# A two-layer hybrid trunk on one core: ten groups of output columns as seven products of quarters, the mixed rows kept as fp32 in DRAM, and weight scales on GpSimd

## The chip, the cores and the metric

The kernel runs on one core of a Trainium2 chip, as one launch. The metric is the device time of that launch in microseconds (us), lower is better. It is the median of 1742.44 us over three runs (1742.14 to 1742.74). The engines are named as the profile names them: PE (TensorE, matmul) with PEld for its weight loads, DVE (VectorE), ACT (ScalarE), POOL (GpSimd) and SP (SyncE, which issues most DMAs).

## The reference

512 tokens with 2048 features go through two layers. Each layer normalises the tokens, makes one combined input projection of 7696 columns, runs three branches on pieces of it, multiplies each branch by its own SiLU gate, joins the three (512 + 1024 + 512 = 2048 columns) and adds one output projection to the residual.

```python
def _layer(x, norm_g, w_in, conv_w, ..., w_out):
    h = _rmsnorm(x, norm_g)
    proj = h @ w_in                                   # 512 x 7696
    y_conv = _short_conv(...) * silu(cv_g)            # 512 columns
    q, k = _rmsnorm(sb_q), _rmsnorm(sb_k)             # 8 heads of 128
    y_sb = _stick_breaking(q, k, v) * silu(sb_g)      # 1024 columns
    g = log_sigmoid(gl_lr @ gla_w_up + gla_b_up) / 16
    y_gla = _rmsnorm(_gla(q, k, v, g)) * silu(gl_g)   # 512 columns
    mix = concatenate([y_conv, y_sb, y_gla])
    return x + mix @ w_out                            # w_out: 2048 x 2048

# stick breaking, per head and block of 128 queries
z = q @ k.T / sqrt(128)
log_keep = where(mask, log_sigmoid(-z), 0)
later = reverse_cumsum(log_keep) - log_keep
w = where(mask, exp(log_sigmoid(z) + later), 0)
out = w @ v
```

The result must be close to fp32. Every large product is therefore made of three fp16 products: with a = a_hi + a_lo and b = b_hi + b_lo, a·b is taken as a_hi·b_hi + a_hi·b_lo + a_lo·b_hi. The halves are fp16, and a power of two per tensor (or per block) brings them into range first.

## The kernel before

**Weight groups.** `specs` lists 76 groups of 256 weight columns in the order in which they are used: per layer 30 of the input projection (six for GLA, four for the first half of the convolution, four each for the four pairs of attention heads, four for the second half of the convolution) and 8 of the output projection. Everything is a pipeline over that list. `weights()` takes the group that PE will use now, lets SP fetch the group after next (`fetch`: two halves of 1 MB, fp32, into the `stage` pool) and prepares the next one (`load_`): ACT squares each half and sums it (`wmax`, L319), GpSimd adds the sums over the partitions (`wgm`, L329), DVE makes a power of two of that in four to six operations on one column (`wscale`, L330 to L350), ACT writes the high half `wh` in fp16 (L392), and DVE writes the rest `wl` (L399). Two 16-bit tiles per half, three halves in the pool.

**Matmuls of a group.** `project_toks` (L568 to L570 are its sister by columns, L576 to L578 the matmuls by tokens) keeps a block of 128 tokens x 128 features as the stationary operand and streams 256 weight columns: 4 token tiles x 16 feature blocks x 3 products = 192 matmuls of 256 columns in one group. `project_cols` gives 96 matmuls of 512 columns. Both use two PSUM banks of `psp`, which has three. The last group of each layer goes token tile by token tile (`project_by_token`, L601), as do the two GLA value groups.

**Branches.** While PE works on a group, ACT, DVE and GpSimd do the branch of earlier groups. GLA comes first and leaves most work to DVE. In attention, one iteration of the loop over j handles two heads and four groups (V, gate, Q, K). The scores and values of pair j are put into `later` and are called one by one between the groups of pair j+1 (`go()`). Per chunk of 128 x 896 or 128 x 384 scores, DVE runs L958, L959, the running sums L962, L965 and L970. `gate` (L609 to L620) copies a PSUM bank to SBUF on ACT first, and so frees the bank.

**Mix.** Each branch result is split into fp16 halves at once (`mixsplit`, L647 and L648) with a scale of its own branch, into two tiles `mh`, `ml`. The output weights then take eight ratios of scales (`wsr`, L347), so each half of a group's weights is made in four pieces of 128 x 512.

**Output groups.** Group `gi` takes the residual rows (`rt`), adds the scaled PSUM bank to them (L1078), writes the sum and, in layer 0, sums its squares on ACT (L1084) for the next layer's norm. The transposed fp16 tokens of the next layer come from `xprep`, as the last group's token tiles land.

**Order.** In the first 40 us the order on DVE and ACT is the program's own. After that a scheduler with a model of the times sets the order on each engine once, when the kernel is built; `high_priority` and `issue_after` are hints to it. On the chip, each engine runs its list in that order and waits for semaphores.

Of the kernel before, what the change touches and what calls it, by code (L numbers as in the profile page):

```python
# [17 lines left out]
P = 128  # L18
EPS = 1e-6
TAU = 16.0  # L20
XBITS = 8.0
RED = bass_isa.ReduceOp

# [7 lines left out]
CHUNKS = ((((3, 0), (2, 512)), (3, 2)), (((0, 0), (1, 128)), (0, 1)))  # L31


@with_exitstack
def hybrid_trunk(ctx, tc, x, norm_g, w_in, conv_w, conv_b, sb_qn_g, sb_kn_g,
# [10 lines left out]
    GX = GW + LR  # L46
    NG = D // GW
# [37 lines left out]
    xs = dram.tile([seq, D], F32, tag="xs", name="xs")  # L85
    xt = [newbig("x", [P, 2, D], F32) for _ in range(2)]
# [22 lines left out]
    parno = wk([P, 32], "raw", 1)  # L109
# [39 lines left out]
    r = 0  # L149
# [90 lines left out]

    V.tensor_scalar(xsc.bitcast(I32), xun.bitcast(I32), -1.0, float(254 << 23), ALU.mult, ALU.add)
# [30 lines left out]
    specs = []  # L272
    for l in range(depth):
        for cols in ([(GL_V, GW)], [(GL_V + GW, GW), (GL_LR, LR)], [(GL_Q, GW)], [(GL_K, GW)],
                     [(GL_G, GW)], [(GL_G + GW, GW)]):
            specs.append((l, w_in, cols))
        conv = [[(l, w_in, [(c0 + j * GW, GW)]) for c0 in (CV_H, CV_C, CV_G, CV_B)] for j in range(2)]
        specs += conv[0]
        for j in range(4):
            for c0 in (SB_V, SB_G, SB_Q, SB_K):  # L280
                specs.append((l, w_in, [(c0 + j * GW, GW)]))
        specs += conv[1]
        for gi in range(NG):
            specs.append((l, w_out, [(gi * GW, GW)]))
# [10 lines left out]
    def junk(n):  # L295

        return wk([P, HK * GX], "junk", 1, dt=U8)[:, :n]


    def fetch(i):  # L300

        l, src, cols = specs[i]
        staged[i] = st = []
        for h in range(2):
            s_ = stage.tile([P, HK, GX], F32, tag="st", name=nm("st"))
            o = 0
            for c0, w in cols:
                nc.sync.dma_start(
                    s_[:, :, o:o + w],
                    src[l, h * HK * P:(h + 1) * HK * P, c0:c0 + w].rearrange("(k p) n -> p k n", p=P))  # L310
                o += w
            st.append(s_)

    def wmax(i, h):

        n = sum(c[1] for c in specs[i][2])
        if h == 0:
            peak[i] = sm(2, "wm")
        S.activation(junk(HK * n).rearrange("p (k n) -> p k n", k=HK), staged[i][h][:, :, :n], AF.Square,  # L319
                     accum_out=peak[i][:, h:h + 1])  # L320

    def wscale(i):

        l, src, cols = specs[i]

        m = sm(1, "wq")
        if i:
            gm = sm(2, "wgm")
            G.partition_all_reduce(gm, peak.pop(i), P, RED.add)  # L329
            V.tensor_scalar(m, gm[:, 0:1], gm[:, 1:2], 2.0 ** -120, ALU.add, ALU.max)  # L330
        else:
# [5 lines left out]
            V.tensor_scalar(m, ps, 2.0 ** -120, None, ALU.max)  # L337
        V.tensor_scalar(m.bitcast(I32), m.bitcast(I32), 0x7F000000, None, ALU.bitwise_and)
        sc = sm(1, "ws")
        V.tensor_scalar(sc.bitcast(I32), m.bitcast(I32), -0.5, float(204 << 23), ALU.mult, ALU.add)  # L340
        p2 = sm(1, "wp")
        V.tensor_scalar(p2.bitcast(I32), m.bitcast(I32), 0.5, float(50 << 23), ALU.mult, ALU.add)
        u = sm(1, "wu", bufs=6)
        sw = None
        if src is w_out:
            sw = sm(8, "wsr")
            V.tensor_scalar(sw, ratio[l][0], sc, None, ALU.mult)  # L347
            V.tensor_tensor(u, p2, ratio[l][1], ALU.mult)
        else:
            V.tensor_tensor(u, p2, xun[:, l:l + 1], ALU.mult)  # L350
        loaded[i] = ([], u)
        scales[i] = (sc, sw)

    def wparts(i, h):
        sc, sw = scales[i]
        return [(slice(2 * j, 2 * j + 2), sw[:, h * 4 + j:h * 4 + j + 1]) for j in range(4)] \
            if sw is not None else [(slice(0, HK), sc)]
# [13 lines left out]

    def whi0(h, q, eng):

        if q == 0:
            wh = wpool.tile([P, HK, GX], F16, tag="wh", name=nm("wh"))
            wl = wpool.tile([P, HK, GX], F16, tag="wl", name=nm("wl"))
            loaded[0][0].append((wh, wl))
        wh = loaded[0][0][h][0]
        ks = slice(q * (HK // 2), (q + 1) * (HK // 2))
        if eng is S:  # L380
            S.activation(wh[:, ks, :GW], staged[0][h][:, ks, :GW], AF.Copy, scale=scales[0][0])
        else:
            V.tensor_scalar(wh[:, ks, :GW], staged[0][h][:, ks, :GW], scales[0][0], None, ALU.mult)

    lasthi = {}

    def whi(i, h):
        n = sum(c[1] for c in specs[i][2])
        wh = wpool.tile([P, HK, GX], F16, tag="wh", name=nm("wh"))
        wl = wpool.tile([P, HK, GX], F16, tag="wl", name=nm("wl"))  # L390
        for ks, s_ in wparts(i, h):
            lasthi[i] = S.activation(wh[:, ks, :n], staged[i][h][:, ks, :n], AF.Copy, scale=s_)  # L392
        loaded[i][0].append((wh, wl))
# [735 lines left out]
```

## Time and profile before

| | us |
|---|---|
| median of three runs (range) | 1742.44 (1742.14 to 1742.74) |
| span of the profiled execution, clock 1.00 throughout | 1740.9 |
| PE busy | 1726.8 (99%) |
| PEld busy | 1232.4 (71%) |
| ACT busy | 1090.0 (63%) |
| DVE busy | 1068.9 (61%) |
| POOL busy | 75.1 (4%) |
| DMA | 204.7 MB, 118 GB/s |

The span is cut by time into GLA (40 to 280 us), attention and second half of the convolution (280 to 735), output groups (735 to 880), the change of layers (880 to 900), and the same again to the end. The table of groups gives a line's busy time, its count and the mean time of one; matmuls are pipelined, so the mean of one (273 ns for 256 columns) is not the spacing of two. The spacing is read from a long stream in the chain of waits.

### The profile page before, as it was taken

To read this page: it belongs to the slowest core of one execution; us is meant where nothing else is said; L and a number is where in the kernel's file an instruction comes from. 1 tells how busy PE (TensorE), PEld (TensorE's weight loads), DVE (VectorE), ACT (ScalarE), POOL (GpSimd) and SP (SyncE) were. 2 spreads that over 40 slices of the span, in tenths; PEclk is the share of its full clock that TensorE was granted. 3 is DMA by queue.
4 is the path that set the end of the run, shared out by engine and by line. 5 is a ranking of instruction groups with operands and counts; after the bars stand their busy time and mean duration, and the time that the engine had idled before them with its cause. 6 is when DMAs were issued, how large, how long until landed. Compare 5 with 4: busy or idle time off the path is not lost.

```text
span 1740.9 us, 30651 instructions
## 1 busy us (share of the span) xinstructions
PE 1726.8 (99%) x12846; PEld 1232.4 (71%) x12846; DVE 1068.9 (61%) x2015; ACT 1090.0 (63%) x1460; POOL 75.1 (4%) x104
## 2 busy tenths in 40 slices
PE   8999999999999999999999999999999999999999
PEld 6744556868787754788885455668686868448888
DVE  7556788657665747433474576976575666673431
ACT  7558577667575867455555684766767667663540
POOL 1000000000000000000010000000000000000000
PEclk9999999999999999999999999999999999999999
DMA  6333313335353545444463333133454444453531
GB/s 222 121 97 97 98 58 113 103 104 131 108 140 110 128 121 128 134 158 146 138 148 105 97 97 97 50 121 110 125 124 109 117 124 126 112 132 113 177 124 40
DMA packets 266121, 204.69 MB, mean 118 GB/s; under 512 B 93106, under 2 KB 265212, under 8 KB 265472
## 3 DMA queue, kind: packets, MB, share of 16 engines
q1 hardware_dynamic: 256976, 193.29, 39.0%
q10 hardware_dynamic: 9008, 9.45, 1.6%
q8 instruction: 100, 1.64, 0.4%
q14 instruction: 37, 0.30, 0.1%
HBM read 173.36 MB, written 8.39 MB: 104 GB/s over the span
## 4 chain that ended last, share of the span: by engine, by line
PE 48%; issue 7%; DVE 1%; DMA 1%; SPq 0%; POOL 0%; ACT 0%; POOLq 0%; DVEq 0%
PE psp L576 8%; PE psp L578 8%; PE psp L577 8%; PE psp L570 6%; PE psp L568 6%; PE psp L569 6%; PE psp L601 3%; PE psz L749 1%; PE psm L988 1%; PE psz L944 1%; PE psz L840 0%; DMA m<-raw 0%; DVE wl L399 0%; SPq L487 0%; DMA xs<-x 0%
## 5 line engine op out<-in xcount | busy, mean ns | idle before, releaser
L577 PE MATMUL psp<-wl,m 128*128 128x256 f16 x1664 | 454.0, 273 | 0.0
L578 PE MATMUL psp<-wh,m 128*128 128x256 f16 x1664 | 453.9, 273 | 0.0
L576 PE MATMUL psp<-wh,m 128*128 128x256 f16 x1664 | 453.8, 273 | 0.0
L399 DVE SCALAR_TENSOR_TENSOR wl<-st,ws,wh 128x2048 f16<-128x2048 f32 (+1 forms) x120 | 282.3, 2353 | 193.1 <-ACT wh L392 179.7
L392 ACT ACTIVATE wh<-st,ws 128x2048 f16<-128x2048 f32 (+1 forms) x118 | 236.3, 2003 | 202.6 <-PE psp L569 100.9
L319 ACT ACTIVATE junk<-st 128x2048 uint8<-128x2048 f32 (+1 forms) x150 | 285.5, 1903 | 7.6 <-DMA st<-in_w_out_dram 4.5
L577 PE MATMUL psp<-wl,x 128*128 128x256 f16 x768 | 209.5, 273 | 0.0
L578 PE MATMUL psp<-wh,x 128*128 128x256 f16 x768 | 209.5, 273 | 0.0
L576 PE MATMUL psp<-wh,x 128*128 128x256 f16 x768 | 209.4, 273 | 0.0
L570 PE MATMUL psp<-m,wl 128*128 128x512 f16 x512 | 194.4, 380 | 0.0
L568 PE MATMUL psp<-x,wh 128*128 128x512 f16 x512 | 194.4, 380 | 0.0
L569 PE MATMUL psp<-x,wh 128*128 128x512 f16 x512 | 194.4, 380 | 0.0
L569 PE MATMUL psp<-m,wh 128*128 128x512 f16 x512 | 194.4, 380 | 0.0
L568 PE MATMUL psp<-m,wh 128*128 128x512 f16 x512 | 194.4, 380 | 0.0
L570 PE MATMUL psp<-x,wl 128*128 128x512 f16 x512 | 194.3, 380 | 0.0
L570 PEld LDWEIGHTS <-wl 128*128 128x128 f16 x1024 | 100.1, 98 | 122.8 <-issue 3.7
L569 PEld LDWEIGHTS <-wh 128*128 128x128 f16 x1024 | 100.1, 98 | 117.5 <-issue 1.1
L568 PEld LDWEIGHTS <-wh 128*128 128x128 f16 x1024 | 100.1, 98 | 115.3 <-issue 0.5
L576 PEld LDWEIGHTS <-m 128*128 128x128 f16 x1664 | 162.7, 98 | 19.9 <-issue 0.7
L578 PEld LDWEIGHTS <-m 128*128 128x128 f16 x1664 | 162.6, 98 | 19.4 <-issue 0.5
L577 PEld LDWEIGHTS <-m 128*128 128x128 f16 x1664 | 162.6, 98 | 18.8
L392 ACT ACTIVATE wh<-st,wsr 128x512 f16<-128x512 f32 x128 | 81.6, 710 | 100.5 <-PE psp L578 74.4
(285 smaller groups left out, 2260.4 us busy)
## 6 DMA issues: line engine op xcount, KB each, us to landing
st<-in_w_in_dram SPq DMA_DIRECT2D x120, 1024.0 KB, 5.3
st<-in_w_out_dram SPq DMA_DIRECT2D x32, 1024.0 KB, 5.5
x<-in_x_dram SPq DMA_DIRECT2D x4, 1024.0 KB
qT<-in_x_dram ACTq DMA_DIRECT2D x8, 512.0 KB, 5.3
qT<-xs ACTq DMA_DIRECT2D x8, 512.0 KB
xs<-x SPq DMA_DIRECT2D x14, 256.0 KB, 4.5
out_dram<-kT SPq DMA_DIRECT2D x14, 256.0 KB, 3.7
th<-za SPq DMA_TRANSPOSE x64, 3.6
```

What stands on the lines that cost most here:

```text
L319: S.activation(junk(HK * n).rearrange("p (k n) -> p k n", k=HK), staged[i][h][:, :, :n], AF.Square, accum_out=peak[i][:, h:h + 1])
L392: lasthi[i] = S.activation(wh[:, ks, :n], staged[i][h][:, ks, :n], AF.Copy, scale=s_)
L399: V.scalar_tensor_tensor(wl[:, ks, :n], staged[i][h][:, ks, :n], s_, wh[:, ks, :n], ALU.mult, ALU.subtract)
L568: T.matmul(o, wh[:, kk, cs], xh[:, :, k, :], start=st_, stop=False)
L569: T.matmul(o, wh[:, kk, cs], xl[:, :, k, :], start=False, stop=False)
L570: T.matmul(o, wl[:, kk, cs], xh[:, :, k, :], start=False, stop=en)
L576: T.matmul(o, ah[:, t, k, :], wh[:, kk, :n], start=st_, stop=False, skip_group_check=True)
L577: T.matmul(o, ah[:, t, k, :], wl[:, kk, :n], start=False, stop=False, skip_group_check=True)
L578: T.matmul(o, al[:, t, k, :], wh[:, kk, :n], start=False, stop=en, skip_group_check=True)
L601: T.matmul(o[:, :n], a_[:, t, k, :], w[k // HK][part][:, k % HK, :n], start=i == 0 and k == 0, stop=i == 2 and k == KT - 1)
L749: T.matmul(o, src16[sb][a][:, ss], tgt16[tb][b][:, g0:g1].rearrange("p g h c -> p (g h c)"), start=i == 0, stop=i == 2)
L944: T.matmul(z[:, o:o + (t + 1) * P], qT[:, a_, t, hh, :], kT[:, b_, :t + 1, hh, :], start=i == 0 and o % 512 == 0, stop=False, skip_group_c ...
```

## The change

**Seven products.** In both layers the output groups 2 to 6 are computed as 2 x 2 blocks: 256 tokens x 1024 features on the left, 1024 features x 128 columns on the right. With sums of the blocks on both sides, seven block products give what eight did. One product is 2 token tiles x 8 feature blocks x 3 fp16 products = 48 matmuls of 128 columns, a group is 336 of them.

- `right(i)` makes seven weight tiles from the staged fp32 quarters a, b, c, d: four sums or differences on DVE (128 x 1024 each, in place), and for each tile the high half on ACT and the rest on DVE.
- `mix_sums` makes, once per layer, four left-hand sums from the fp32 mix, and their halves.
- `seven` runs the products and combines them on the way out of PSUM, with two temporaries (`u2`, `vv`) and one copy (`s1`).

```diff
+SEVEN = {"gla": (), "conv0": (), "sb": (), "conv1": (), "out": (2, 3, 4, 5, 6)}
...
-    stage = ctx.enter_context(tc.tile_pool(name="stage", bufs=3))
-    wpool = ctx.enter_context(tc.tile_pool(name="wpool", bufs=3))
-    big = ctx.enter_context(tc.tile_pool(name="big", bufs=4))
+    stage = ctx.enter_context(tc.tile_pool(name="stage", bufs=4))
+    wpool = ctx.enter_context(tc.tile_pool(name="wpool", bufs=6))
+    big = ctx.enter_context(tc.tile_pool(name="big", bufs=2))
...
+    def right(i):
...
+        part(a)
+        V.tensor_tensor(b, b, d, ALU.add)
+        V.tensor_tensor(a, a, b, ALU.add)
+        part(a)
+        part(c)
+        V.tensor_tensor(c, c, a, ALU.add)
+        V.tensor_tensor(a, a, d, ALU.subtract)
+        part(a)
+        part(b)
+        part(d)
+        part(c)
...
+        product(o1, 0, True, False)
+            S.activation(s1, o1[:, :2 * P], AF.Copy, scale=ev.unit)
+        product(o2, 1, True, True)
+            ev.add(u2, o2[:, :2 * P], s1)
+        product(o1, 2, False, True)
+        ev.first(o1[:, :2 * P])
+        product(o3, 3, True, True)
+            ev.sub(vv, o3[:, :2 * P], u2)
+        product(o4, 4, True, False)
+        ev.last4(vv, o4[:, :2 * P])
+        product(o2, 5, True, True)
+        ev.plus(0, 1, o2[:, :2 * P], vv)
+        product(o4, 6, False, True)
+        ev.plus(1, 0, o4[:, :2 * P], u2)
```

On DVE, in layer 0, this is the work of about half an output group (group 4 before, group 4 after). First before: the lower halves of the weights, eight pieces, and the group's two evictions.

```order
L399 SCALAR_TENSOR_TENSOR wl_8339<-st_8066,wsr_8335,wh_8338 128x2x256 [waits DMAHW6_49,Activation_49]
L399 SCALAR_TENSOR_TENSOR wl_8339<-st_8066,wsr_8335,wh_8338 128x2x256 [waits Activation_49] x3
L399 SCALAR_TENSOR_TENSOR wl_8349<-st_8068,wsr_8335,wh_8348 128x2x256 [waits DMAHW7_49,Activation_49]
L399 SCALAR_TENSOR_TENSOR wl_8349<-st_8068,wsr_8335,wh_8348 128x2x256 [waits Activation_49] x3
L1078 SCALAR_TENSOR_TENSOR x_7557<-psp_8358,wu_8084,qT_8314 128x2x256 [waits DMAHW5_49,PE_49]
L1078 SCALAR_TENSOR_TENSOR x_7558<-psp_8359,wu_8084,qT_8314 128x2x256 [waits PE_49]
```

After, on DVE: `st` are the staged weights (L433 is the first sum b + d of the next group, L434 the second), `w` the lower halves, and L1340 to L1362 the combinations on the way out of PSUM.

```order
L433 TENSOR_TENSOR st_8495<-st_8495,st_8497 128x8x128 [waits DMAHW6_49,DMAHW5_49,Activation_49]
L1360 TENSOR_TENSOR qT_8903<-u_1003_9048,qT_8903 128x2x128 [waits DMAHW4_49,DVE_49]
L430 SCALAR_TENSOR_TENSOR w_8526<-st_8085,ws_8509,w_8526 128x1024 [waits Activation_49]
L430 SCALAR_TENSOR_TENSOR w_8529<-st_8085,ws_8509,w_8529 128x1024 [waits Activation_49]
L1348 SCALAR_TENSOR_TENSOR x_7581<-psp_8948,wu_8511,qT_8903 128x2x128 [waits PE_49]
L430 SCALAR_TENSOR_TENSOR w_8532<-st_8087,ws_8509,w_8532 128x1024 [waits Activation_49]
L430 SCALAR_TENSOR_TENSOR w_8535<-st_8087,ws_8509,w_8535 128x1024 [waits Activation_49]
L1343 SCALAR_TENSOR_TENSOR vv_9148<-psp_9099,wu_8511,u_1003_9048 128x256 [waits PE_49]
L1354 TENSOR_TENSOR qT_8903<-vv_9148,qT_8903 128x2x128 [waits DVE_49]
L1360 TENSOR_TENSOR qT_8903<-vv_9148,qT_8903 128x2x128
L1356 SCALAR_TENSOR_TENSOR x_7582<-psp_9150,nu_9199,qT_8903 128x2x128 [waits DVE_49,PE_49,Pool_49]
```

The first sum of the next group (L433) now stands ahead of the lower halves of the present one, and it waits for ACT, which squares the next group's weights; before, nothing on DVE stood between a group's lower halves and its evictions.

**Weight scales on GpSimd.** The five operations on one column move from DVE to GpSimd, with fp32 arithmetic in place of the bit mask. Before, on DVE, for one output group:

```order
L330 TENSOR_SCALAR wq_8325<-wgm_8326 128x1 [waits Pool_49]
L338 TENSOR_SCALAR wq_8325<-wq_8325 128x1 [waits DVE_49]
L340 TENSOR_SCALAR ws_8330<-wq_8325 128x1 [waits DVE_49]
L342 TENSOR_SCALAR wp_8332<-wq_8325 128x1
L347 TENSOR_SCALAR wsr_8335<-ratio_7385,ws_8330 128x8 [waits DVE_49]
L348 TENSOR_TENSOR wu_8334<-wp_8332,rgm_7380 128x1 [waits DVE_49]
```

After, on POOL, for one output group. [...]

```order
L348 ISA
L348 ISA wgm_9325<-wm_9319 128x2 [waits Activation_49]
L352 ISA
L352 TENSOR_SCALAR wq_9324<-wgm_9325 128x1 [waits Pool_49]
L361 TENSOR_SCALAR wq_9324<-wq_9324 128x1 [waits Pool_49]
L363 TENSOR_SCALAR ws_9329<-wq_9324 128x1 [waits DVE_49,Pool_49]
L365 TENSOR_SCALAR wu_9331<-wq_9324,rub_7378 128x1
L1352 TENSOR_SCALAR nu_10006<-wu_9331 128x1 [waits DVE_49,Pool_49]
```

POOL's list grows from 109 rows to 610, with one change of library before the change and 154 after it.

```diff
     def wscale(i):
...
-            V.tensor_scalar(m, gm[:, 0:1], gm[:, 1:2], 2.0 ** -120, ALU.add, ALU.max)
+            E = G
+            E.tensor_scalar(m, gm[:, 0:1], gm[:, 1:2], 2.0 ** -120, ALU.add, ALU.max)
...
-        V.tensor_scalar(m.bitcast(I32), m.bitcast(I32), 0x7F000000, None, ALU.bitwise_and)
+        E.tensor_scalar(m, m.bitcast(I32), 2.0 ** -24, MAGIC, ALU.mult, ALU.add)
...
+        E.tensor_scalar(sc.bitcast(I32), m, -(2.0 ** 23), (MAGIC + 204) * 2.0 ** 23, ALU.mult, ALU.add)
```

**Mix in DRAM.** `spill` writes each branch row block (128 x 512 fp32, 256 KB) to `mixd` in DRAM; `mix_load` brings twelve of the sixteen back before the last projection of the layer, and the last four stay in SBUF. `mix_unit` makes one scale for all, `mix_split` the fp16 halves, into the same two tiles that held the normalised tokens. With one scale, the ratios `wsr` and their eight pieces per group go.

```diff
-    def mixsplit(k, y, s_, t0=0):
...
+        def spill(k, y):
+            nc.sync.dma_start(mixd[k], y)
...
+        LATE = (10, 11, 2, 3)
+        for k in (0, 4, 6, 8, 12, 14, 10, 2):
+            mix_split(k, s_)
+        if any(modes[cursor[0]:cursor[0] + NG]):
+            sums = mix_sums(s_)
```

**Attention.** The running sum now takes both terms, so per chunk DVE runs one scan per query tile and two operations instead of four. The values of the second head of pair j move by one iteration (`held`).

```diff
-                    V.scalar_tensor_tensor(w, w, -1.0, a, ALU.mult, ALU.subtract)
-                    V.scalar_tensor_tensor(a, z[:, :zw], zs, w, ALU.mult, ALU.subtract)
-                    for t, o in qtiles:
-                        back = a[:, o:o + (t + 1) * P][:, ::-1]
-                        V.tensor_tensor_scan(back, ones.to_broadcast([P, (t + 1) * P]), back, 0.0,
-                                             ALU.mult, ALU.add)
-                    V.tensor_tensor(w[:, :zw - 1], w[:, :zw - 1], a[:, 1:], ALU.subtract)
+                    for t, o in qtiles:
+                        grow_, keep_ = (x[:, o:o + (t + 1) * P][:, ::-1] for x in (w, a))
+                        V.tensor_tensor_scan(keep_, grow_, keep_, 0.0, ALU.add, ALU.add)
+                    V.scalar_tensor_tensor(w, z[:, :zw], zs, a, ALU.mult, ALU.subtract)
...
+            prior = held.pop() if held else lambda: None
+            if j < 3:
+                held.append(lambda: values(1))
+                later.extend((lambda: scores(0), prior, lambda: scores(1), lambda: values(0)))
```

On ACT, at the start of the third pair of heads (j = 2), layer 0. Before, the two banks of V leave PSUM (L1011) ahead of the softmax of the pair before:

```order
L1011 ACTIVATE v_4965<-psp_4771 128x512 [waits PE_49]
L392 ACTIVATE wh_5045<-st_4743,ws_5039 128x8x256 [waits DVE_49,PE_49]
L1011 ACTIVATE v_4965<-psp_4772 128x512
L952 ACTIVATE za_4984<-psz_4975,zun 128x896 [waits DMAHW7_49,PE_49]
L956 ACTIVATE zw_4988<-psz_4975,nzun 128x896
```

After, they leave (L1233) behind the softmax (L1171 to L1183) and behind the first column block of the gate (L809):

```order
L1180 ACTIVATE zw_4974<-zw_4974 128x896 [waits DVE_49]
L809 ACTIVATE ga_5138<-psp_5038,nu_5136 128x512 [waits PE_49]
L1183 ACTIVATE za_4970<-zw_4974 128x896 [waits Activation_49]
L1233 ACTIVATE v_4953<-psp_4759 128x512 [waits PE_49]
L1233 ACTIVATE v_4953<-psp_4760 128x512
L811 ACTIVATE ga_5138<-ga_5138 128x512 [waits DVE_49]
```

L1233 waits for PE: the tile `v` has two buffers, and the held values of pair j-2 still read the older one.

**Gate.** `gate` takes exp, ln and exp from the PSUM bank (three ACT operations for five) and multiplies from the bank too (L813), so a bank is held until DVE's last operation on it.

More of the change, by code (lines that the diff above doesn't have):

```diff
@@ L519, in hybrid_trunk @@
     xlow(0, 1, mix, True)
-    wlo(0, 0)
-    wlo(0, 1)
+    for q in range(4):
+        wlo(0, q)
     xhigh(1, 0, mix)
@@ new lines, in project_toks @@
+    def project_toks(late=()):
+        w, u = weights()
+        ps = [bank(psp, "p") for _ in range(2)]
+        rounds = [[k for k in range(h * HK, (h + 1) * HK) if k not in late] for h in range(2)] + [list(late)]
+        lastk = [q for q in rounds if q][-1][-1]
+        for ks in rounds:
+            for t in range(NT):
+                o = ps[t // 2][:, (t % 2) * GW:(t % 2 + 1) * GW]
+                for k in ks:
+                    wh, wl = (wview(w, i, k, GW) for i in range(2))
+                    T.matmul(o, xh[:, k, t, :], wh, start=k == 0 and t % 2 == 0, stop=False, skip_group_check=True)
+                    T.matmul(o, xh[:, k, t, :], wl, start=False, stop=False, skip_group_check=True)
+                    T.matmul(o, xl[:, k, t, :], wh, start=False, stop=k == lastk, skip_group_check=True)
+        return ps, u
@@ new lines, in project_by_token, with quarters, own @@
+    def project_by_token(n):
+        w, u = weights()
+        for t in range(NT):
+            o = bank(psp, "p")
+            for i, (a_, part) in enumerate(((xh, 0), (xl, 0), (xh, 1))):
+                for k in range(KT):
+                    T.matmul(o[:, :n], a_[:, k, t, :], wview(w, part, k, n),
+                             start=i == 0 and k == 0, stop=i == 2 and k == KT - 1)
+            yield t, o, u
+    def quarters(sums):
+        def own(th, kh):
+            return [a[:, kh * HK:(kh + 1) * HK, 2 * th:2 * th + 2, :] for a in mix]
+        return own(0, 0), sums[1], own(0, 1), sums[0], sums[2], sums[3], own(1, 1)
```

597 lines of the change are left out of this document (384 added, 213 removed).

## The prediction

> **What bounds the kernel now.** I read the page's busy times first, then the windows by stage, then the chain of waits for the spacing of matmuls, and last the timeline of one output group.
>
> ```profile
> PE 1726.8 (99%) x12846; PEld 1232.4 (71%) x12846; DVE 1068.9 (61%) x2015; ACT 1090.0 (63%) x1460; POOL 75.1 (4%) x104
> PEclk9999999999999999999999999999999999999999
> ```
>
> ```profile
> 280.00:700.00 420.00, 420.00 (x3161) 303.39 (x3160) 275.15 (x468) 283.43 (x351) 19.51 (x26) 1.00 0.45 118
> 735.00:860.00 125.00, 125.00 (x1147) 111.92 (x1146) 48.45 (x99) 67.33 (x123) 2.39 (x6) 1.00 0.51 161
> 880.00:900.00 20.00, 17.22 (x156) 15.10 (x154) 17.54 (x29) 11.49 (x16) 3.91 (x2) 1.00 0.63 130
> 1720.00:1740.90 20.90, 17.29 (x159) 15.24 (x156) 1.94 (x4) 0.00 (x0) 0.00 (x0) 0.99 0.08 26
> ```
>
> PE is busy for 1726.8 of 1740.9 us, at full clock. In the windows (span, PE, PEld, DVE, ACT, POOL) it has no gap in attention (420 of 420 us) nor in the output groups (125 of 125); it stands still for 2.8 us at the change of layers and 3.6 us in the last window, the rest at the start. So time falls only where PE has less to do, and rises wherever another engine makes PE wait. Work taken from DVE or ACT is worth nothing by itself.
>
> ```profile
> 1015.49 1.34 PE psz L749 x24
> 1160.34 3.32 PE psz L840 x48
> 1228.90 0.65 PE psz L944 x3
> 1229.61 0.49 PE psz L944 x3
> 1274.29 1.65 PE psm L988 x18
> 1716.33 20.97 PE psp L601 x192
> 1737.33 0.48 DVE kT L1078
> ```
>
> The chain gives spacings: 192 matmuls of 256 columns take 20.97 us, 109.2 ns each. 24 matmuls of 128 columns take 1.34 us, 55.8 ns each. The 48 of L840 are 36 of 128 columns and 12 of 256, and 36 × 55.8 + 12 × 109.2 ns = 3.32 us agrees. Matmuls of 512 columns come every 0.216 us (thirteen steps between these two rows of the timeline), 48 of them take 10.4 us:
>
> ```profile
> 299.81 0.38 PE L569 MATMUL psp<-x,wh 128*128 128x512 f16 x1
> ...
> 302.62 0.38 PE L570 MATMUL psp<-x,wl 128*128 128x512 f16 x1
> ```
>
> **Seven products: the gain.** 336 × 55.8 ns = 18.75 us against 20.97 us, 2.22 us per group. Ten groups: **-22.2 us**. That the spacing holds over 336 matmuls rather than 24 is not in the trace; it is the first thing that can fail (rival A).
>
> **Seven products: what else must fit into 18.75 us.**
>
> ```profile
> L1054 DVE SCALAR_TENSOR_TENSOR qp<-raw,qp 128x1024 f16<-128x1024 f32 x16 | 19.6, 1226 | 18.0 <-ACT qp L1053 18.0
> L1053 ACT ACTIVATE qp<-raw 128x1024 f16<-128x1024 f32 x16 | 16.9, 1057 | 44.0 <-DVE raw L1049 25.8 <-DVE raw L1044 18.1
> L319 ACT ACTIVATE junk<-st 128x2048 uint8<-128x2048 f32 (+1 forms) x150 | 285.5, 1903 | 7.6 <-DMA st<-in_w_out_dram 4.5 <-DMA st<-in_w_in_dram 1.2
> L995 DVE SCALAR_TENSOR_TENSOR e<-psm,vu,g 128x256 f32<-128x256 f32 x32 | 13.9, 476 | 0.0
> L735 DVE TENSOR_TENSOR m<-e,m 128x256 f16<-128x256 f32 x32 | 13.4, 423 | 7.8 <-ACT m L734 7.3
> L1084 ACT ACTIVATE junk<-x 128x256 uint8<-128x256 f32 x32 | 13.3, 416 | 65.8 <-DVE x L1078 65.0 <-ACT junk L1084 0.3
> ```
>
> DVE: 11 operations of 128 x 1024 (seven lower halves, four sums) at 1.23 us, six evictions at 0.48 and three small sums at 0.42, together 17.6 us; neighbours in the timeline overlap by about 0.09 us, so about 15.8. ACT: seven high halves at 1.06, two squares of weights at 1.90 and their read-outs at 0.19, `s1` and, in layer 0, four squares of the result at some 0.6, together 12 to 14.4. Both fit, DVE with 1 to 3 us to spare. What counts is the order. From group 3 on, DVE's sum b + d of the next group stands ahead of the lower halves of tiles 4 to 7 of the present one, and it waits for ACT's square of the next weights. From the start of a group: product 1 ends at 48 × 55.8 ns = 2.68 us, `s1` 0.42, a square 0.5 (layer 0), the weights' square 2.1, the sum 1.22, a small sum 0.33, the lower half 1.14: 8.4 us, where product 4 wants that tile at 3 × 2.68 = 8.04. So PE waits about 0.4 us per group in layer 0 and nothing in layer 1, if the scale of the weights is no later than before.
>
> ```profile
> 822.95 0.19 ACT L319 ACTIVATION_READ_ACCUMULATOR junk<-st 128x1 f32 x1
> 824.61 2.56 ACT L392 ACTIVATE wh<-st,wsr 128x512 f16<-128x512 f32 x4 [1.48 <-DVE wu L348]
> 828.35 2.74 DVE L399 SCALAR_TENSOR_TENSOR wl<-st,wsr,wh 128x512 f16<-128x512 f32 x4 [0.24 <-ACT wh L392]
> 838.07 0.75 DVE L1078 SCALAR_TENSOR_TENSOR x<-psp,wu,qT 128x512 f32<-128x512 f32 x1 [4.49 <-PE psp L578]
> ```
>
> Before, the scale took 1.48 us (the end of the second square to the first high half), and the weights were complete at 831.1, seven us ahead of the group's end at 838. In the seven groups that lead is gone: the tiles of the next group need buffers that free one by one.
>
> **The scale on GpSimd.**
>
> ```profile
> 0.73 0.10 POOL L133 MEMSET avg<- 128x1 f32 x1 [0.29 <-POOLq L1115]
> L169 POOLq MODIFY_POOL_CONFIG  x2: 11/11/11, 30.3 to 30.3; - x2
> 30.40 0.73 POOL L169 PARTITION_ALL_REDUCE kgm<-kg  x2
> 411.59 2.35 DVE L399 SCALAR_TENSOR_TENSOR wl<-st,ws,wh 128x2048 f16<-128x2048 f32 x1
> 412.60 3.06 POOL L329 PARTITION_ALL_REDUCE wgm<-wm  x1 [21.40 <-ACT junk L319]
> 413.85 1.56 DVE L965 TENSOR_TENSOR zw<-zw,za 128x895 f32<-128x895 f32 x2
> L81 ACT ACT_TABLE_LOAD x1 | 1.3, 1283 | 0.7 <-PEq L1115 0.7
> ```
>
> The trace has no arithmetic on one column on POOL. The nearest rows are a memset of one column (0.10 us) below and the sum over partitions (0.37 us, two in 0.73) above, so three dependent operations up to the scale cost 0.3 to 1.1 us beside the sum itself. They can also be held up: the sum that starts at 412.60 lasts 3.06 us, as long as DVE's run of operations with two SBUF inputs from 411.59 to 415.4. [...] In the seven groups such DVE operations are 1.2 us long and fill two thirds of the time, and each step of the chain can meet one. I take 3 us for the scale instead of 1.5, with 1 and 4.5 as ends. ACT's first high half waits for it, then everything behind; walked like the path above, PE waits for what exceeds some 2.3 us in layer 0 (groups 3 to 6: about 0.8 us each) and 2.7 in layer 1 (0.3 each). Sum **+4.4 us**, ends 0 and, at 4.5 us, some 16. Elsewhere the delay is covered:
>
> ```profile
> 419.51 2.35 DVE L399 SCALAR_TENSOR_TENSOR wl<-st,ws,wh 128x2048 f16<-128x2048 f32 x1 [0.75 <-ACT wh L392]
> 429.12 2.00 ACT L392 ACTIVATE wh<-st,ws 128x2048 f16<-128x2048 f32 x1 [1.83 <-PE psp L578]
> ```
>
> After that late scale, the first half of the weights was ready at 421.9, and the second waited for PE to free a buffer until 429.1; PE lost nothing.
>
> The change of library, 154 times, is costed by its only row: 11 ns, with the next operation 0.1 us behind it, so nothing. Whether that row shows a real load or one that found its code in place, the trace can't say; the upper bound is the longest stay of any POOL operation that waits, 3.06 us, with the load of ACT's tables (1.28 us) between (rival D).
>
> **Attention.** DVE loses two operations of some 0.8 us per chunk and ACT two of 0.63 per gate block; PE had no gap there, so nothing. The new wait is at V of pairs 2 and 3 in both layers: V's two banks leave PSUM only after the held values (tile `v` has two buffers). PE runs column block 0 of the gate, the values (1.65 us, row 1274.29), a score chunk (0.65 and 0.49 us by the rows of L944, with two masks of 0.06: 1.25), and then needs a bank for column block 1.
>
> ```profile
> L1011 ACT ACTIVATE v<-psp 128x512 f16<-128x512 f32 x16 | 9.3, 580 | 0.1
> L1012 DVE SCALAR_TENSOR_TENSOR v<-psp,v 128x512 f16<-128x512 f32 x16 | 10.9, 682 | 0.0
> xs<-x SPq DMA_DIRECT2D x14, 256.0 KB, 4.5
> ```
>
> From the end of the values: 0.1 us to ACT, 0.58, 0.1 to DVE, two of 0.68, and an operation of 0.82 on DVE ahead that may run into it: 2.1 to 2.9 us, less the 1.35 of the score chunk. I take 1.0 us at each of four places: **+4 us**, ends 2 (half of it) and 10 (ACT or DVE late by one more operation).
>
> **The rest.** The gate now holds a bank until DVE's multiplication, about 2 us longer; a third bank and 10.4 us per column block cover it, and without that cover it costs up to 2 us at each of 20 gates. `spill` and `mix_load` add 24 pieces of 256 KB per layer to SP's queue, among the fetches of weights: 12.6 MB on 204.7, DMA at 45% in attention, 4.5 us each to land against fetches that run two groups ahead. Nothing, unless a piece that waits for its data holds a fetch behind it. The splits and sums at the start of the output groups run while PE is in groups 0 and 1, which put the late rows last. The change of layers keeps its form: +1 us, between -2.8 (its idle time gone) and +2.8 (doubled).
>
> **Sum.** -22.2 + 4.4 + 4 + 1 = -12.8. The span of 1740.9 becomes 1728.1; the median of the runs lies 1.5 us above the profiled span, so **about 1730 us**; with the ends above its own range is 1721 to 1741.
>
> **Rivals.**
>
> *A: the long stream of short matmuls is slower.*
>
> ```profile
> L749 PEld LDWEIGHTS <-m 128*128 128x128 f16 x432 | 30.4, 98 | 9.6
> ```
>
> Each matmul of 128 columns brings a weight load, which lasts 98 ns by its row. If loads don't overlap fully over 336 pairs, the spacing lies between 55.8 and 98 ns. It decides from 20.97 / 336 = 62.4 ns on. Midway, at 77 ns, a group takes 25.9 us and ten cost +49 us: about 1791. For it: nothing longer than 24 is shown. Against it: 24 loads in 1.34 us already overlap.
>
> [...]
>
> *B: the gain is clean.* Nothing waits: 1742.4 - 22.2 = 1720. For it: attention hid a scale that was 2.65 us late. Against it: the walks above come out late by themselves, if only by 0.4 and 1 us.
>
> *C: VectorE and the banks eat it.* Waits between the middle and their upper ends: at the upper ends -22.2 + 16 + 10 + 2.8 = +6.6, so about 1738 to 1749.
>
> *D: each change of library is a real load in the chain.* One stands between the sum over partitions and the first arithmetic (the other lies ahead of a wait and is hidden). With 3 us, the scale takes 6; PE waits for all of what exceeds some 2.3 us, 3.7 us at each of eight groups (3 to 6, both layers), +30 us, plus 5 for V and layers: -22.2 + 30 + 5 = +13, 1755. From 1.6 us per load it is slower than before. In attention ACT would stand 3 us more in each group of some 21 us, and it has 6.8 idle there (283 of 420 busy). For it: the two kinds of operation alternate 75 times. Against it: the row above, 0.1 us.
>
> [...]
>
> **How the numbers follow.** Forecast 0.45, B 0.13, C 0.12, D 0.20, A 0.10. A change of 0.2%, 3.5 us, is what can be told here. Faster: forecast, B and 0.02 of C, 0.60. Same: 0.07 of C and 0.02 of D, 0.09. Slower: 0.03 of C, 0.18 of D, A, 0.31. The range reaches from 1719, below B, to 1785, over most of D and the lower end of A.
>
> **What would show it.** In the profile after: PE's chain should have streams of 336 matmuls in 18.7 to 18.8 us (A wrong); PE's idle time in groups 3 to 6 should be under 2 us each and released by DVE's lower halves or ACT (C); the time from the second square of weights to the first high half should be 2 to 4 us, and POOL should show no gap of microseconds between the sum and the first one-column operation (D); V's second bank should hold PE about 1 us at four places; PE's idle time in all some 24 us (14 before, 9.4 more). A spacing above 62 ns, or a scale later than 5 us, makes the forecast wrong.

## The result, and the profile after

The changed kernel takes 1850.85 us (median of four runs, 1849.74 to 1853.46), the kernel before, on the same chip, 1742.59. The ratio is 1.0624 (95% interval 1.0609 to 1.0639): 108 us slower, where 12 us faster was forecast. The profiled execution has a span of 1849.7 us.

The page of the changed kernel, busy times and the granted clock in 40 slices:

```profile
PE 1738.6 (94%) x14286; PEld 1251.0 (68%) x14286; DVE 1108.2 (60%) x1724; ACT 1120.4 (61%) x1502; POOL 202.9 (11%) x452
PEclk9999999999999999988978999999999999999999
```

PE is idle for 111 us (14 before), and it is busy for 12 us more, although it has 22 us less to do: in the slices of the first layer's output groups and of the change of layers the clock falls (the digits 8, 8, 9, 7, 8 in the row above). DVE and ACT are no busier than before, as shares. So neither is the bound; PE waits for something that is not work.

The timeline of POOL in one output group of layer 0 (start, duration, operation, idle time before it and what ended that):

```profile
800.06 0.88 POOL L348 PARTITION_ALL_REDUCE wgm<-wm  x1 [17.99 <-ACT junk L335]
809.81 0.31 POOL L352 TENSOR_SCALAR wq<-wgm 128x1 f32<-128x1 f32 x1 [8.87 <-issue]
810.21 0.19 POOL L361 TENSOR_SCALAR wq<-wq 128x1 f32<-128x1 int32 x1
810.48 0.19 POOL L363 TENSOR_SCALAR ws<-wq 128x1 int32<-128x1 f32 x1
```

Between the sum over partitions (ends at 800.94) and the first operation on one column lie 8.87 us in which POOL waits for no other engine ("issue"). In POOL's list the row `ISA` without operands stands there, in the profile a row MODIFY_POOL_CONFIG of 83 ns (146 of them, below); "change of library" is the name for it here. What it does inside POOL no view shows; its place and the time behind it were measured. The three operations up to the scale then take 0.86 us. Over the program, in the table of POOL's waits (in total, times, longest):

```profile
POOL wq L352 <- issue: 539.7, 73, 9.4
```

539.7 us in 73 places, 7.4 us each. ACT sees it as this, in the timeline of the same group and in the table of its waits:

```profile
799.73 0.19 ACT L335 ACTIVATION_READ_ACCUMULATOR junk<-st 128x1 f32 x1
810.70 1.15 ACT L429 ACTIVATE w<-st,ws 128x1024 f16<-128x1024 f32 x1 [10.78 <-POOL ws L363]
```

```profile
ACT w L429 <- POOL ws L363: 56.5, 7, 11.3
ACT w L412 <- POOL ws L363: 32.1, 4, 16.5
...
ACT w L410 <- POOL ws L363: 16.1, 2, 9.2
```

From the last square of the weights to the first high half it takes 10.8 us; it was 1.48 before, and 3 were forecast. PE stands behind that. In this group the low half on DVE follows the high half, and DVE's eviction L1356, which frees PE's bank, follows the low half; it ends at 813.6. Two rows of PE's table of waits:

```profile
PE psp L669 <- ACT w L429: 13.2, 5, 4.9
PE psp L669 <- DVE x L1356: 8.8, 1, 8.8
```

When PE starts again it is slow. In the chain of waits and in one window (the column behind the busy times is the granted clock):

```profile
801.01 8.79 issue
813.62 8.30 PE psp L669 x96
```

```profile
813.00:823.00 10.00, 9.38 (x119) 9.38 (x120) 7.42 (x9) 5.11 (x12) 0.00 (x0) 0.68 0.33 106
```

The 96 matmuls of 128 columns take 86 ns each instead of 55.8: after the gap the clock is 0.68 in that window.

### The profile page after: what moved, and what is told of

The parts are those of the page before. It is cut to its first block, busy times and chain, and to the rows that moved or that the text cites. A ratio compares the mean times of both kernels' runs of the same rounds, so it can differ in the third digit from the quotient of the medians.

```text
span 1849.7 us, 34097 instructions
## 1 busy us (share of the span) xinstructions
PE 1738.6 (94%) x14286; PEld 1251.0 (68%) x14286; DVE 1108.2 (60%) x1724; ACT 1120.4 (61%) x1502; POOL 202.9 (11%) x452
## 4 chain that ended last, share of the span: by engine, by line
PE 66%; DVE 11%; issue 10%; ACT 8%; DMA 2%; POOL 1%; ACTq 0%; POOLq 0%; SPq 0%; DVEq 0%
PE psp L614 10%; PE psp L615 10%; PE psp L616 10%; PE psp L632 8%; PE psp L630 8%; PE psp L631 8%; PE psp L642 5%; ACT junk L335 3%; PE psp L669 3%; ACT w L429 2%; DVE w L430 2%; DVE w L416 1%; PE psz L932 1%; DVE act L1069 1%; DMA st<-in_w_out_dram 1%
## 5 line engine op out<-in xcount | busy, mean ns | idle before, releaser
L630 PE MATMUL psp<-w,act 128*128 128x256 f16 x1792 | 490.1, 273 | 5.9 <-DVE kT L1320 5.9
L632 PE MATMUL psp<-w,act 128*128 128x256 f16 x1792 | 489.9, 273 | 1.7 <-DVE act L1069 1.5
L631 PE MATMUL psp<-w,act 128*128 128x256 f16 x1792 | 489.9, 273 | 0.0
L416 DVE SCALAR_TENSOR_TENSOR w<-st,ws,w 128x1024 f16<-128x1024 f32 x264 | 335.4, 1280 | 217.6 <-ACT w L412 217.0
L412 ACT ACTIVATE w<-st,ws 128x1024 f16<-128x1024 f32 x260 | 295.7, 1144 | 254.6 <-PE psp L632 105.7
L614 PE MATMUL psp<-act,w 128*128 128x512 f16 x1024 | 389.4, 380 | 0.0
L616 PE MATMUL psp<-act,w 128*128 128x512 f16 x1024 | 389.4, 380 | 0.0
L615 PE MATMUL psp<-act,w 128*128 128x512 f16 x1024 | 389.3, 380 | 0.0
L335 ACT ACTIVATE junk<-st 128x2048 uint8<-128x2048 f32 x150 | 285.1, 1900 | 9.1 <-DMA st<-in_w_in_dram 7.9
L631 PEld LDWEIGHTS <-act 128*128 128x128 f16 x1792 | 175.9, 98 | 28.0 <-issue 6.7
L632 PEld LDWEIGHTS <-act 128*128 128x128 f16 x1792 | 175.9, 98 | 24.5 <-DVE act L1069 3.0
L630 PEld LDWEIGHTS <-act 128*128 128x128 f16 x1792 | 175.9, 98 | 21.6
L616 PEld LDWEIGHTS <-w 128*128 128x128 f16 x1024 | 100.5, 98 | 120.0 <-issue 2.0
L614 PEld LDWEIGHTS <-w 128*128 128x128 f16 x1024 | 100.5, 98 | 119.4 <-issue 3.8
L615 PEld LDWEIGHTS <-w 128*128 128x128 f16 x1024 | 100.6, 98 | 119.1 <-issue 4.7
L642 PE MATMUL psp<-w,act 128*128 128x256 f16 (+1 forms) x1152 | 144.3, 288 | 36.9 <-ACT w L412 16.6
L642 PEld LDWEIGHTS <-act 128*128 128x128 f16 x1152 | 117.2, 102 | 61.6 <-issue 20.4
L429 ACT ACTIVATE w<-st,ws 128x1024 f16<-128x1024 f32 x70 | 77.0, 1140 | 108.8 <-POOL ws L363 56.5
L430 DVE SCALAR_TENSOR_TENSOR w<-st,ws,w 128x1024 f16<-128x1024 f32 x70 | 88.0, 1281 | 70.0 <-ACT w L429 70.0
L669 PE MATMUL psp<-w,act 128*128 128x128 f16 x1440 | 93.7, 229 | 30.0 <-ACT w L429 12.6
L352 POOL TENSOR_SCALAR wq<-wgm 128x1 f32<-128x1 f32 x75 | 52.1, 695 | 539.9 <-issue 539.7
```

Source lines behind the costliest of these rows:

```text
L335: S.activation(junk(HK * GW).rearrange("p (k n) -> p k n", k=HK), staged[i][h], AF.Square, accum_out=peak[i][:, h:h + 1])
L412: his.setdefault(i, []).append(S.activation(quarter(i, q, 0)[:, :, :GW], staged4(i, q), AF.Copy, scale=scales[i]))
L416: V.scalar_tensor_tensor(lo[:, :, :GW], staged4(i, q), scales[i], hi[:, :, :GW], ALU.mult, ALU.subtract)
L430: V.scalar_tensor_tensor(lo, x, scales[i], hi, ALU.mult, ALU.subtract)
L614: T.matmul(o, wh, xh[:, k, :, :], start=st_, stop=False)
L615: T.matmul(o, wh, xl[:, k, :, :], start=False, stop=False)
```

## The experiments

### The one-column operations back on DVE; no seven products; both; and the kernel before with its scales on GpSimd

```diff
# e1_scale_on_dve: the changed kernel, with
-            E = G
+            E = V
-            G.tensor_scalar(nu, u, -1.0, None, ALU.mult)      # and uu, vu, u2, the third sum likewise
+            V.tensor_scalar(nu, u, -1.0, None, ALU.mult)
# e2_no_seven: the changed kernel, with
-"out": (2, 3, 4, 5, 6)}
+"out": ()}
# e3_no_seven_scale_on_dve: both
# e4_before_scale_on_gpsimd: the kernel before, with wscale's arithmetic as
+            E = G
+            E.tensor_scalar(m, gm[:, 0:1], gm[:, 1:2], 2.0 ** -120, ALU.add, ALU.max)
+        E.tensor_scalar(m, m.bitcast(I32), 2.0 ** -24, MAGIC, ALU.mult, ALU.add)
...
```

> The changed kernel with every one-column operation back on DVE; GpSimd keeps only the sums over partitions and its memsets, so its library changes fall from 154 to 2. Theory D (a library change is a real load of 7 to 9 us in the chain of each weight group): the whole loss goes, 1722 to 1741 us, clock 1.00 throughout. Theory A (the long stream of 128-column matmuls is slow by itself): the ten groups stay as they are, above 1780, with 336 matmuls in over 21 us and PE without gaps. Theory C (VectorE and the banks): 1738 to 1750.

> The changed kernel with no group in seven products (its output groups have 192 matmuls of 256 columns again); the scales stay on GpSimd. Theory D: the output groups have about 7 us of lead, so they lose little, but the loads still cost at the start of each layer, where PE waits in the changed kernel too (about 9 and 25 us) and in the rest: 1775 to 1800. Theory A: with the short matmuls gone the loss goes, 1740 to 1750.

> No seven products and the one-column operations on DVE: what is left are the mix in DRAM, the held values, the gate and the running sum. Theory D with the sum of the prediction: 1743 to 1748 (V +4, layers +1). The difference to the run with seven products and scales on DVE is the net gain of seven products: 13 to 22 us by the prediction, below 5 by theory C, negative by theory A.

> The kernel before with only the arithmetic of the weight scales moved to GpSimd (seven small operations for each group). Theory D: a wait of 7 to 9 us between the sum over partitions and the first of them in every group; hidden where a group has lead, seen where it has none (starts of layers, ACT held up in its queue): 1765 to 1800. Theories A and C: nothing in this kernel depends on them, 1742 to 1746.

| | median, us | ratio to before (95%) |
|---|---|---|
| changed kernel | 1850.85 | 1.0624 (1.0609 to 1.0639) |
| e1: scales on DVE | 1747.29 | 1.0028 (1.0018 to 1.0037) |
| e2: no seven products | 1800.60 | 1.0328 (1.0311 to 1.0346) |
| e3: neither | 1762.95 | 1.0116 (1.0101 to 1.0132) |
| e4: before, scales on GpSimd | 2069.47 | 1.1869 (1.1851 to 1.1887) |

Expected by theory D were 1722 to 1741 us for e1, 1775 to 1800 for e2, 1743 to 1748 for e3 and 1765 to 1800 for e4: e2 lies at its upper end, the other three are slower than that. e1 lies in the range of theory C (1738 to 1750); what it loses against theory D turned out to be V, below.

Moving the small operations back to DVE returns 103.6 of the 108 us. Theory A falls with the chain of e1, in the second layer's groups 2 to 6:

```profile
1626.87 93.80 PE psp L669 x1680
```

1680 matmuls in one piece, 55.8 ns each: the spacing of the burst of 24 holds over five groups, and PE doesn't wait there once. In layer 0, PE waits for the lower half three times, 0.6 us each (`PE psp L669 <- DVE w L430: 1.8, 3, 0.7` in its table of waits); the walk of the prediction gave 0.4.

Seven products and the library changes make each other worse: the changes cost 103.6 us with seven products (changed kernel less e1), but 37.7 without (e2 less e3). And the kernel before pays most, 327 us, far above what I expected. Its ACT, POOL and PE show a part of why, in two timelines and three rows of the tables of waits:

```profile
535.43 0.41 POOL L330 PARTITION_ALL_REDUCE wgm<-wm  x1 [15.26 <-ACT junk L320]
543.11 0.31 POOL L332 TENSOR_SCALAR wq<-wgm 128x1 f32<-128x1 f32 x1 [7.28 <-issue]
```

```profile
544.01 2.00 ACT L395 ACTIVATE wh<-st,ws 128x2048 f16<-128x2048 f32 x1 [7.57 <-POOL ws L343]
545.92 0.58 ACT L1036 ACTIVATE raw<-psp 128x512 f32<-128x512 f32 x1
```

```profile
ACT wh L395 <- POOL ws L343: 401.4, 56, 13.8
ACT wh L395 <- POOL wsr L350: 166.0, 16, 18.7
PE psp L579 <- ACT raw L1036: 29.5, 10, 3.9
```

ACT stands still for 7.6 us before the high half, and the copy that frees a PSUM bank (L1036) is behind it in ACT's list; PE then waits for the bank. That row is one of several in PE's table there; the longest is for a transposing DMA (kT, 39.9 us). ACT waits 567 us for the scale in 72 places there (the first two rows), 105 us in 13 places in the changed kernel (the three rows above). In the changed kernel the high halves wait longer for PE to free a quarter (209 us in two rows of ACT's table), so the scale has time to arrive; that this difference in order explains the whole gap between 104 and 327 us was not tested.

e1 and e3 left a question. e3 is 20 us slower than before, where the prediction had 5. PE's table of waits in e1 has one row for most of it, and e3 has it too (11.0 us):

```profile
PE psm L1204 <- DVE v L1234: 10.9, 4, 2.8
```

These are the four places of V. One of them, in the timelines of ACT, SP, DVE and PE of e1:

```profile
570.36 1.81 PE L1204 MATMUL psm<-th,v 128*128 128x256 f16 x18
571.88 0.67 ACT L809 ACTIVATE ga<-psp,nu 128x512 f32<-128x512 f32 x1
572.45 0.94 ACT L1183 ACTIVATE za<-zw 128x896 f16<-128x896 f32 x1
573.29 1.07 ACT L1233 ACTIVATE v<-psp 128x512 f16<-128x512 f32 x2
573.41 1.22 SPq L1186 DMA_TRANSPOSE th<-za  x1
575.37 0.68 DVE L1234 SCALAR_TENSOR_TENSOR v<-psp,v 128x512 f16<-128x512 f32 x1
576.17 0.27 PE L1204 MATMUL psm<-th,v 128*128 128x256 f16 x1 [2.75 <-DVE v L1234]
```

ACT could copy V's banks when the held values end at 572.2, but it does the gate (L809) and a high half of the softmax (L1183) first; DVE's part then ends at 576.05. PE waits 2.75 us. But the matmul that waits is not the gate's: it is the first one of the next values, which stands in PE's list ahead of the gate's second column block, and it reads `th`, the transposed softmax weights. The transposing DMA that writes them is issued at 573.41, when L1183 is done, and lands 2.6 us later, at 576.0, at the same time as DVE's part ends. So the releaser in e1's row can be a coincidence. The changed kernel has the same four waits with the other name, and in the last of them the two come apart:

```profile
PE psm L1204 <- DMA th<-za: 11.3, 4, 3.1
1527.81 1.27 DVE L1234 SCALAR_TENSOR_TENSOR v<-psp,v 128x512 f16<-128x512 f32 x2
1529.64 0.37 PE L1204 MATMUL psm<-th,v 128*128 128x256 f16 x1 [3.15 <-DMA th<-za]
```

There DVE was done with V at 1529.1, and PE went on waiting until 1529.64, for the DMA. V's banks were late too: in e1 the first was free at 575.4, so without that matmul PE would have waited some 2.0 us (an estimate from these rows).

The matmuls behind the wait, same timeline of PE of e1:

```profile
578.04 0.64 PE L615 MATMUL psp<-act,w 128*128 128x512 f16 x1
578.47 0.63 PE L616 MATMUL psp<-act,w 128*128 128x512 f16 x1
...
582.06 0.38 PE L615 MATMUL psp<-act,w 128*128 128x512 f16 x1
582.28 0.38 PE L616 MATMUL psp<-act,w 128*128 128x512 f16 x1
```

From 577.5 on, for about 3.4 us, they come every 0.43 us, half the speed of the 0.216 before and after; the granted clock is 0.50 in the window from 578 to 580. So this wait of 2.75 us costs about 1.7 us more. The same happens behind two of the other three waits of e1; behind the one that ends at 1343.55 it doesn't (clock 1.00 in the window from 1340 to 1350, 0.83 in the like windows of the other three).

### The values not held; the same without seven products; GpSimd for the inputs only; the library change beside the chain

```diff
# e7_scale_on_dve_no_hold: e1, with
-            prior = held.pop() if held else lambda: None
-            if j < 3:
-                held.append(lambda: values(1))
-                later.extend((lambda: scores(0), prior, lambda: scores(1), lambda: values(0)))
-            else:
-                later.extend((lambda: scores(0), lambda: (prior(), scores(1)), lambda: values(0), lambda: values(1)))
+            later.extend((lambda: scores(0), lambda: scores(1), lambda: values(0), lambda: values(1)))
# e8_no_seven_no_hold: e7, and "out": ()
# e5_gpsimd_for_inputs_only: the changed kernel, with
-            E = G
+            E = V if src is w_out else G
# e6_library_change_aside: the kernel before, with, behind the sum over partitions,
+            G.tensor_scalar(sm(1, "idle"), gm[:, 0:1], 1.0, None, ALU.mult)
```

> Seven products, one-column operations on DVE, and the values of a pair's second head back in the next pair, as in the kernel before, so that V's tile is free when V's banks are copied out. Theory V (the held values block V's banks; measured four waits of 2.7 to 2.8 us): the four waits go, 1747.3 less 11 to 12, so 1735 to 1737, faster than before by 0.3 to 0.4%. Rival (the wait only moves, to the scores or values of the same pair): 1744 to 1749.

> The same without seven products: what the mix in DRAM, the gate, the running sum and the tiles in quarters cost by themselves. Theory V: 1763 less 11 to 12, 1750 to 1752, of which some 8 us above the kernel before are still to be explained; rival: 1760 to 1764. The difference to the run with seven products is their gain: 14 to 18 us.

> The changed kernel with the scales of the output weights on DVE and those of the input weights still on GpSimd. It splits the 104 us of the library changes. Theory (lead decides: seven products have none, the projections have 7 us or more): the output groups give back the larger part, 60 to 75 us, so 1775 to 1790. Rival (each change costs about the same wherever it stands, 104 / 75 = 1.4 us, and 16 of 75 are output groups): 1850 less 22, about 1828.

> The kernel before with one more operation on GpSimd behind each sum over partitions, whose result nobody reads: as many library changes as in the changed kernel, but none between the sum and the scale. Theory (the place in the chain costs, not the load itself): 1742 to 1746, with the loads seen in GpSimd's idle time. Rival (the loads disturb by their own traffic, or hold up other engines): more than 1760.

| | median, us | ratio to before (95%) |
|---|---|---|
| e7: scales on DVE, values not held | 1730.63 | 0.9932 (0.9919 to 0.9944) |
| e8: the same, no seven products | 1745.79 | 1.0017 (1.0008 to 1.0027) |
| e5: GpSimd for input weights only | 1782.04 | 1.0226 (1.0210 to 1.0241) |
| e6: before, library changes aside | 1774.25 | 1.0179 (1.0165 to 1.0193) |

Only e5 lies in the range that its theory gave: e7 and e8 are some 4 us faster than expected, and e6 lies in the range of its rival.

**V.** Without the held values the four waits are gone, and e7 is the fastest kernel here, 11.9 us below the kernel before. It gains 16.7 us over e1, more than the 11 of the waits themselves. e7 undoes the held order as a whole, so it doesn't tell V's banks from the DMA. The page of e7 and its window of attention:

```profile
PE 1706.3 (99%) x14286; PEld 1233.0 (71%) x14286; DVE 1155.4 (67%) x2080; ACT 1120.0 (65%) x1502; POOL 52.8 (3%) x96
300.00:720.00 420.00, 419.69 (x3153) 304.20 (x3152) 251.13 (x426) 278.56 (x350) 7.71 (x19) 1.00 0.48 131
```

The gain of 16.7 us is made up of 10.9 us of waits, 5.1 us of slow matmuls behind three of them (1.7 each) and 0.6 us by which e7 is ahead at 40 us already (a wait of PE at the start ends at 39.4 instead of 40.1). Without seven products the same edit gives 17.2 us (e3 to e8).

**Seven products** are worth 15.2 us (e8 less e7), of the 22.2 of the matmuls alone. PE's waits in the two kernels name two parts of the rest: the three waits of 0.6 us in layer 0, and the transposing DMA at the change of layers, 4.2 us against 1.6 (and the clock is 0.91 behind it from 880 to 900, 1.00 in e8, which is some 1.7 us more):

```profile
PE psp L642 <- DMA act<-qp: 4.2, 2, 3.2
PE psp L669 <- DVE w L430: 1.8, 3, 0.7
```

**Where the library changes cost.** e5 stands 34.7 us above e1 and 68.8 below the changed kernel. So the scales of 16 output groups carry two thirds. A price for each change wherever it stands (1828 expected) is excluded. The other third is not the 59 input groups alone: e5 keeps the small operations of the branches on GpSimd, and the sign of the unit (`nu`) in the output groups. The first and last start of the matmuls of groups 2 to 6 show how the loss is spread, changed kernel first, then e1 (layer 0, layer 1):

```profile
L669 PE MATMUL psp<-w,act x720: 216/219/314, 782.7 to 923.0; 128*128 128x128 f16 x180
L669 PE MATMUL psp<-w,act x720: 216/219/219, 1724.9 to 1825.1; 128*128 128x128 f16 x180
L669 PE MATMUL psp<-w,act x720: 216/219/220, 765.8 to 862.1; 128*128 128x128 f16 x180
L669 PE MATMUL psp<-w,act x720: 218/219/220, 1626.7 to 1720.5; 128*128 128x128 f16 x180
```

The five groups take 140.3 us against 96.3 in layer 0, and 100.2 against 93.8 in layer 1: a loss of 44 and of 6 us. In layer 1 the scale mostly comes in time: from 1660 us on ACT's high halves for the seven products (L429) wait for it 4.1 us in two places, against 52.3 us in five between 740 and 1000. Before the first scores (L1163) 11 us are lost, and 31 between group 6 and the first scores of layer 1. In e5 the five groups of layer 0 still take 104.3 us, 8 more than in e1, with the scales on DVE and `nu` on GpSimd.

**Beside the chain.** e6 has two library changes per group, neither between a sum and its scale. I expected no loss; it is 32 us, which by its number fits the rival. Its windows (span, PE, PEld, DVE, ACT, POOL, clock) say where:

```profile
40.00:160.00 120.00, 111.51 (x638) 64.83 (x637) 62.05 (x141) 67.31 (x75) 9.10 (x14) 0.96 0.28 88
290.00:500.00 210.00, 210.00 (x1663) 159.27 (x1662) 139.02 (x242) 143.27 (x183) 13.64 (x22) 1.00 0.41 115
740.00:890.00 150.00, 150.00 (x1377) 134.44 (x1375) 59.06 (x122) 80.07 (x144) 5.14 (x14) 1.00 0.48 150
890.00:1000.00 110.00, 98.76 (x667) 66.81 (x665) 55.70 (x107) 52.66 (x67) 13.38 (x12) 0.95 0.40 107
```

Attention and the output groups lose nothing: 210 of 210 and 150 of 150 us, with changes of library in every group. So the changes cost PE nothing there, and their place in a chain is what costs. The loss is at the starts of the layers (the first and the last of these windows, and the first 40 us), where POOL's sums follow each other too closely. Its timeline there:

```profile
101.12 0.41 POOL L329 PARTITION_ALL_REDUCE wgm<-wm  x1 [5.86 <-ACT ga L683]
109.32 1.41 POOL L331 TENSOR_SCALAR idle<-wgm 128x1 f32<-128x1 f32 x1 [7.79 <-issue]
118.30 0.37 POOL L169 PARTITION_ALL_REDUCE qTgm<-qTmx  x1 [7.58 <-issue]
```

This pair of changes takes 15.4 us of POOL, 17.2 with its two operations. The input of the sum for q's scale, which the branch waits for, was ready at 108.1 (DVE L704); the sum came at 118.3. A gap of more than 7 us stands in front of each of the two operations.

## Why the prediction was wrong, step by step

- **The step that failed** is "The change of library, 154 times, is costed by its only row: 11 ns, with the next operation 0.1 us behind it, so nothing." Each change in front of the arithmetic took 7.4 us (539.7 us in 73 places). Why the one change before cost 0.1 us no run shows. I said that the trace couldn't tell, and then took the lower value. It alone turns the forecast: 103.6 us of 108.
- **Its upper bound failed too.** Rival D had the right place, a wait in the chain of the scale, but took at most 3 us per change from the longest POOL row, and so 1755. With the measured 10.8 us for the scale, its own rule (PE waits for what exceeds 2.3 us, eight groups) gives 68 us, and e5 gives back 68.8; that they agree is luck. The rule counts both layers alike, but groups 2 to 6 lose 44 us in layer 0 and 6 in layer 1, and more is lost at the change of layers, which the rule leaves out. What was measured is 6.8 to 9.4 us, shown as idle time with the reason "issue". The range ended at 1785.
- **The 3 us for the scale without a change** (+4.4 us in the sum) were my estimate from one sum of 3.06 us, and no run shows them. In the changed kernel the longest of the 75 sums of the weights lasted 1.36 us, and the first operation behind it 0.31 to 2.40, 0.31 in most places.
- **"Elsewhere the delay is covered"** was said of 3 us, which no run tests; with 7 us and more it failed: some 27 us of e5's 34.7 are lost outside its output groups. The cover was counted for the weights; ACT's list, with other work behind the high halves, was not counted (rival D's 6.8 us of idle time of ACT per group, a mean over a window, hid that order). e4 shows one such place.
- **Seven products: the gain** of 2.22 us per group was right (55.8 ns over 1680 matmuls), and rival A wrong. The stalls in layer 0 were 0.6 us at three groups (0.4 walked, with a scale as before), in layer 1 none, as walked.
- **V** had the right four places and the right cause, the held values, but the wait that ended last was another, and the size was wrong: 1.0 us at each place was forecast, 2.75 was measured, and 16.7 us in all by e7. I walked V's two banks only, with ACT free when the values ended; it was 1.1 us late there, with DVE behind it, and the first bank came free after some 2.0 us. The wait of 2.75 us is for the transposing DMA of the softmax weights (2.6 us from its issue), which the walk left out, as it left out the matmul that waits for it. A third of the 16.7 us is the clock, which I had not in the sum at all.
- **The rest** (gate, mix in DRAM, running sum, +1 us): e8, which has these and neither of the three above, stands 3.3 us over the kernel before.
- **The number 1730** is met by e7 (1730.63), but by luck and not by the forecast's sum: that had +4 for V and -17.8 for seven products with their stalls, where e7 has no V and -15.2, and +3.3 for the rest.

## What to carry to other kernels

Before small arithmetic is moved to an engine that is mostly idle, look in its list for what stands between its kinds of work: here a change of library between the sum over partitions and the arithmetic on GpSimd, with 7.4 us of idle time behind it (73 places of the changed kernel), in a chain that took 1.48 before. A row that shows a cost of nothing for something that happens once is no price for doing it 154 times in alternation; the bound must then be as wide as the place can bear. A wait in front of PE can cost more than its length: behind three of e1's four waits of 2.7 us the clock that PE is granted halved for 3.4 us. And the releaser that a row names may only be the one that happened to end last: look at what the waiting instruction reads (here `th`) and at the same wait in another run.

## What the runs showed of the hardware

- A change of library between a sum over partitions and arithmetic goes with an idle time of POOL of 6.8 to 9.4 us in front of the arithmetic (the changed kernel's 73 places) and, where it shows, 5.7 to 8.0 us in front of a sum (7.58 us at 118.30 in e6). Memsets of POOL show no such gap: one starts at 66.55 in the changed kernel right behind arithmetic, one at 42.04 in the kernel before, 0.64 us behind a sum and released by DVE. The two sides look different in the trace, 83 ns for the row in front of arithmetic and 11 ns for the one in front of a sum, and neither row holds the gap:

```profile
L352 POOLq MODIFY_POOL_CONFIG  x146: 82/83/83, 57.8 to 1805.4; - x146
L348 POOLq MODIFY_POOL_CONFIG  x140: 5/11/12, 51.0 to 1794.9; - x140
```

- Arithmetic on one column takes GpSimd 0.19 to 0.31 us (changed kernel, the group from 809.81 on), a little more than DVE takes (0.14 to 0.22, kernel before, the group from 823.66 on).
- After waits of 2.72 to 2.75 us, PE ran at half speed for about 3.4 us (0.43 us for 512 columns), from 0.6 to 1.3 us behind the wait on, in three of e1's four places and in one of three in the changed kernel; what decides it is open. Of the changed kernel's 121 us over e7 some 21 are this: matmuls at half clock took 24.6 us longer than at full clock there, 3.1 in e7. PE's busy time, 1738.6 against 1706.3 us with the same matmuls, differs by more.
- Matmuls of 128 columns with a weight load each keep 55.8 ns over 1680 pairs (e1).
